# Seven block products for eight in three FFN up-projections (fp32), and FFN down in one pass over eight PSUM banks

## The chip, the cores and the metric

The kernel runs on one core of one Trainium2 chip. The metric is the device time of one execution in microseconds, the median of 3 runs. The engines are called as the profile calls them: PE is TensorE, with PEld its weight loads; DVE is VectorE, ACT is ScalarE, POOL is GpSimd, and SP is the engine whose queue issues the DMAs.

## The reference

Two transformer blocks, the second of two layers, on 512 tokens of width 1024, all in fp32. What the change touches is the feed-forward part, which occurs three times: FFN 0 at the end of the first block, FFN 1 and FFN 2 in the second one, these two with a causal convolution over 3 tokens between.

```
# FFN 0 (D_FF = 2816)
n2 = rmsnorm(h, norm_ffn_pre)
gu = n2 @ w_ffn_in                                  # [512,1024] @ [1024,5632]
ff = (silu(gu[:, :D_FF]) * gu[:, D_FF:]) @ w_ffn_out
h = h + rmsnorm(ff, norm_ffn_post)

# FFN 1 and 2
u = h_normed @ w_up                                 # [512,1024] @ [1024,5632]
y = conv_b + sum(u_padded[j : j + 512] * conv_w[j] for j in range(3))
gate, up = split(y, 2)
x = x + (silu(gate) * up) @ w_down                  # [512,2816] @ [2816,1024]
```

## The kernel before

Every fp32 operand of a matmul is kept as two parts of 12 bits (`split`: ScalarE writes the high part by a copy, VectorE the low part as the difference). A product of two such pairs is `mm3`, three matmuls (lines 108 to 110) into one PSUM bank: high by high, high by low, low by high. The normed and transposed activations X are two tiles, XH and XL, of 8 blocks of 128 channels by 512 tokens.

`projA` computes 256 features of X @ w, feature-major, in two banks: two loads of 512 KB into `raw` (2 buffers), two splits into `whi` and `wlo` (4 buffers each, `RING`), and 16 mm3 of 512 columns. In FFN 0 the split also multiplies by the norm's gain (`split_scaled`, four pieces of 256 a load). A *block* is what one projA computes, and a *pair* f the gate block and the up block of features f and f + 1 (of 22 groups of 128); an FFN has 11 pairs. `gate_sink` and `up_sink` take the results out of the banks: the convolution (`mixed`: one instruction on ScalarE, two on VectorE), silu, the product, and its split into FH and FL, 22 by 512 each. The first pair of each FFN goes through `projA_first`, whose matmuls have 256 columns, so that the last two token tiles are needed late.

`out_proj` is the down projection: `projB` computes the first 512 output columns for all token tiles, in the four rotating banks ("pj"), over 11 chunks of 256 features; then a second pass computes the other 512 columns in the banks c0 to c3, and its last four chunks are taken token tile by token tile, so that `finish` (the residual, the next norm and its transposes) of one tile runs beside the matmuls of the next.

Instructions are issued to in-order queues, one an engine; the framework that builds the program may place an instruction ahead of others of its engine where data and buffers allow. So an eviction that waits for a bank holds up what stands behind it on ScalarE or VectorE. All loads are issued by SP.

## Time and profile before

| | us |
|---|---|
| median of 3 runs (2075.93 to 2077.32) | 2075.95 |
| span of the profiled execution | 2073.6 |
| TensorE busy in it | 2043.1 |
| VectorE busy | 1064.8 |
| ScalarE busy | 847.4 |
| pairs 2 to 11 of FFN 1, 20 blocks | 224.0 |

The profile is of one execution, and its own time is known only by its span, from the first to the last instruction; the median lies 2.35 us above that. Matmuls are pipelined: the duration of one is longer than the distance to the next, so rates are read from starts. FFN 0's up-projection runs from about 440 to 680 us, its down projection to 800; FFN 1 follows the HGRN layer, from about 1127 to 1374 and to 1490; FFN 2 follows the MLA layer, from about 1700 to 1948 and to the end.

### The profile page before, as it was taken

The numbers are of one execution on the slowest core, as the hardware profiler recorded it, in microseconds if no ns is written. First come the engines' busy times: TensorE is split into PE (matmuls) and PEld (weight loads), VectorE is DVE, ScalarE is ACT, GpSimd is POOL, SyncE is SP. The second block draws the span as 40 slices with busy tenths as digits, with TensorE's granted clock in tenths as the row PEclk, the third lists the DMA queues.
The fourth block names the chain that finished last, engine by engine and source line by source line (L and its number), as shares of the span: only waits on it lengthen the run. The fifth ranks groups of instructions, "written<-read, shape, count | busy, mean of one in ns | idle before, by whom it ended". The sixth has DMA issues, their size and how long they took to land.

```text
span 2073.6 us, 26103 instructions
## 1 busy us (share of the span) xinstructions
PE 2043.1 (99%) x10225; PEld 1671.8 (81%) x10225; DVE 1064.8 (51%) x1936; ACT 847.4 (41%) x1649; POOL 55.2 (3%) x84
## 2 busy tenths in 40 slices
PE   8999999999999999999999999999999999999999
PEld 6777778888888888888888888888787788888887
DVE  5664543474443225766555665542466456565421
...
GB/s 219 89 90 72 71 77 127 92 102 92 92 93 99 93 94 79 82 71 63 71 42 77 102 97 96 92 92 101 53 107 41 41 53 100 102 92 92 98 116 61
DMA packets 151362, 182.70 MB, mean 88 GB/s; under 512 B 6983, under 2 KB 118854, under 8 KB 151238
## 3 DMA queue, kind: packets, MB, share of 16 engines
...
q14 instruction: 43, 0.35, 0.0%
HBM read 178.90 MB, written 2.10 MB: 87 GB/s over the span
## 4 chain that ended last, share of the span: by engine, by line
PE 92%; DVE 3%; ACT 2%; DMA 1%; POOL 1%; issue 1%; SPq 0%; POOLq 0%; ACTq 0%; DVEq 0%
PE A L108 17%; PE A L109 17%; PE A L110 17%; PE B L108 10%; PE B L110 10%; PE B L109 9%; PE hs L924 2%; PE zt L86 1%; PE tr L86 1%; PE ov L1013 1%; PE mo L1230 1%; PE mz L1204 1%; POOL r L125 1%; PE sbo L450 1%; PE z L427 1%
## 5 line engine op out<-in xcount | busy, mean ns | idle before, releaser
L108 PE MATMUL A<-XH,whi 128*128 128x512 f32 (+1 forms) x1552 | 590.5, 381 | 0.8 <-ACT XH L62 0.8
L109 PE MATMUL A<-XL,whi 128*128 128x512 f32 (+1 forms) x1552 | 585.4, 377 | 1.5 <-DVE XL L65 1.5
L110 PE MATMUL A<-XH,wlo 128*128 128x512 f32 (+1 forms) x1552 | 584.7, 377 | 0.0
L65 DVE TENSOR_TENSOR wlo<-raw,whi 128x1024 fp32r<-128x1024 f32 (+2 forms) x253 | 301.5, 1193 | 451.9 <-ACT whi L62 451.6
L62 ACT ACTIVATE whi<-raw 128x1024 fp32r<-128x1024 f32 (+2 forms) x253 | 262.1, 1036 | 471.9 <-PE B L110 249.0
L110 PEld LDWEIGHTS A<-XH,wlo 128*128 128x128 f32 x1552 | 293.0, 189 | 58.8 <-issue 0.2
L109 PEld LDWEIGHTS A<-XL,whi 128*128 128x128 f32 x1552 | 293.5, 189 | 57.9 <-DVE XL L65 1.9
L108 PEld LDWEIGHTS A<-XH,whi 128*128 128x128 f32 x1552 | 292.8, 189 | 57.9 <-ACT XH L62 1.3
L108 PE MATMUL B<-whi,FH 128*128 128x512 f32 x528 | 207.2, 392 | 0.0
L110 PE MATMUL B<-whi,FL 128*128 128x512 f32 x528 | 207.0, 393 | 0.0
L109 PE MATMUL B<-wlo,FH 128*128 128x512 f32 x528 | 205.9, 390 | 0.0
L62 ACT ACTIVATE whi<-raw,cols 128x256 fp32r<-128x256 f32 (+1 forms) x272 | 126.8, 525 | 175.4 <-PE A L109 92.4
L68 DVE SCALAR_TENSOR_TENSOR wlo<-raw,cols,whi 128x256 fp32r<-128x256 f32 (+1 forms) x272 | 126.7, 512 | 121.6 <-ACT whi L62 121.3
L68 DVE SCALAR_TENSOR_TENSOR y<-A,convc,y 128x511 f32<-128x511 f32 (+1 forms) x176 | 131.7, 748 | 90.5 <-ACT y L62 87.4
L108 PE MATMUL B<-whi,XH 128*128 128x512 f32 (+2 forms) x416 | 165.8, 400 | 0.0
L109 PE MATMUL B<-wlo,XH 128*128 128x512 f32 (+2 forms) x416 | 158.3, 381 | 2.1 <-DVE wlo L65 1.7
L110 PE MATMUL B<-whi,XL 128*128 128x512 f32 (+2 forms) x416 | 158.0, 381 | 0.0
L109 PEld LDWEIGHTS B<-wlo,FH 128*128 128x128 f32 x528 | 99.1, 188 | 22.2
L110 PEld LDWEIGHTS B<-whi,FL 128*128 128x128 f32 x528 | 99.2, 188 | 21.9
L108 PEld LDWEIGHTS B<-whi,FH 128*128 128x128 f32 x528 | 99.2, 188 | 20.7
L62 ACT ACTIVATE y<-A,convc 128x512 f32<-128x512 f32 x88 | 67.7, 770 | 77.4 <-PE A L110 77.4
L110 PEld LDWEIGHTS B<-whi,XL 128*128 128x128 f32 x416 | 78.5, 189 | 14.9 <-DVE XL L65 0.3
...
## 6 DMA issues: line engine op xcount, KB each, us to landing
...
```

Source lines behind the costliest of these rows:

```text
L62: return nc.scalar.activation(out=out_, in_=in_, func=func, **kw)
L65: return nc.vector.tensor_tensor(out=out_, in0=in0, in1=in1, op=op)
L68: return nc.vector.scalar_tensor_tensor(out=out_, in0=in0, scalar=scalar, in1=in1, op0=op0, op1=op1)
L86: nc.tensor.transpose(dst_bank[:, k * P : (k + 1) * P], s_, ident)
L108: nc.tensor.matmul(out_, lhsT=sta[0], rhs=mov[0], start=first, stop=False)
L109: nc.tensor.matmul(out_, lhsT=sta[0], rhs=mov[1], start=False, stop=False)
L110: nc.tensor.matmul(out_, lhsT=sta[1], rhs=mov[0], start=False, stop=last)
L125: nc.gpsimd.tensor_tensor(out=r, in0=v, in1=mhalf[:, :w], op=ALU.pow)
L427: nc.tensor.matmul(z[:, :n], lhsT=qT[u][r, sl], rhs=kT[v][r, :n], start=u + v == 0, stop=False)
L450: nc.tensor.matmul(b[r, :P], lhsT=sv[:, j, c0 : c0 + 64], rhs=A[:, j * P : (j + 1) * P], start=j == 0, stop=j == i,)
L924: nc.tensor.matmul(b[:, sl], lhsT=K[:, e, sl], rhs=Q[:, e, sl], start=True, stop=True)
L1013: nc.tensor.matmul(b[:, e * P : (e + 1) * P], lhsT=l_, rhs=hv[:, j, hd * P : (hd + 1) * P], start=q == 0, stop=q == len(lhs) - 1,)
```

## The change

Strassen's scheme on 2 x 2 x 2 blocks: 256 features are two halves (`i`), the 1024 channels are the even and the odd groups of 128 (`j`), the 512 tokens two halves of 256 (`l`). `seven` computes a block of 256 features by seven products of [128 features, 512 channels] by [512 channels, 256 tokens] in place of eight. Each product is four mm3 with 256 columns. It needs sums of weight quarters (`usum`, four a block, on VectorE, then split like the quarters that are used as they are) and of activation quarters. Those four (nT1, T3, nT2, T4) are computed once an FFN by `x_sums`, from an unsplit copy of X that `norm_T` now writes as well (`plain`, on ScalarE), and kept split as `xc`. The sums of products are formed partly in the banks (bank Y takes four products one after another, each partial sum copied out by ScalarE; bank XZ takes the others) and partly by VectorE into `dst`.

In FFN 0 gate and up blocks of pairs 2 to 11 are done so; in FFN 1 and 2 the gate blocks, with the up block still a projA whose two parts lie between the pieces of the gate block. The generators' yields lay two blocks side by side. The tiles of `whi` and `wlo` become one ring "w" of 8 tiles of the same size; a product takes one, a split of projA two. The weights of a block of seven come in two loads of [1024, 128] instead of [512, 256], as many bytes. FFN 0's norm takes its gain before the transposes (on VectorE) and its weights are split unscaled. FT is one unsplit fp32 tile; `pair_of` splits it chunk by chunk in the down projection, which takes both column halves in one pass over eight banks.

```diff
-    wp = ctx.enter_context(pool("wp", bufs=RING))
+    wp = ctx.enter_context(pool("wp", bufs=2 * RING))
...
     def chunk(src, nk, n, g=None):
-        """A [nk*128, n] block of a weight matrix (its rows times g) as an exact pair of 12-bit parts."""
         raw = wp.tile([P, nk, n], F32, tag="raw", name=nm("raw"), bufs=2)
         load(raw, src.rearrange("(k p) n -> p k n", p=P))
-        hi = wp.tile([P, nk, n], F32R, tag="whi", name=nm("whi"))
-        lo = wp.tile([P, nk, n], F32R, tag="wlo", name=nm("wlo"))
+        hi = wp.tile([P, nk, n], F32R, tag="w", name=nm("whi"))
+        lo = wp.tile([P, nk, n], F32R, tag="w", name=nm("wlo"))
...
+                act(plain[:, hf * 4 : hf * 4 + 4, c0 : c0 + P], b.rearrange("p (k t) -> p k t", k=4), AF.Copy)
 
...
+            if mid is not None and half.start == 0:
+                mid()
...
+    def mmB(bs, t, c, ch, X, nk, n=512, x0=0):
+            xs_ = X[0][:, kk - x0, sl], X[1][:, kk - x0, sl]
+            mm3(bs[t][:, :n], xs_, (hi[:, k], lo[:, k]), kk == 0, kk == nk - 1)
...
+    def halves_of(T, j, l):
+        return T.rearrange("p (c j) t -> p j c t", j=2)[:, j, :, l * 256 : (l + 1) * 256]
+    def x_sums(X, plain, tmp, xp):
+        B = {(j, l): halves_of(plain, j, l) for j in range(2) for l in range(2)}
+        nT1, T3, nT2, T4 = (tmp[:, 2 * i : 2 * i + 2].rearrange("p k (u t) -> p (k u) t", u=2) for i in range(4))
+        ops = {}
+        def parts(key, src):
+            t_ = [xp.tile([P, 4, 256], F32R, tag="xc", name=nm("xc"), bufs=8) for _ in range(2)]
+            split(src, *t_)
+            ops[key] = t_
+        tt(nT1, B[0, 0], B[0, 1], ALU.subtract)
+        parts("nT1", nT1)
+        tt(T3, B[1, 1], B[0, 1], ALU.subtract)
+        stt(nT2, T3, -1.0, B[0, 0], ALU.mult, ALU.subtract)
+        parts("nT2", nT2)
+        parts("T3", T3)
+        stt(T4, nT2, -1.0, B[1, 0], ALU.mult, ALU.subtract)
+        parts("T4", T4)
+        for j, l in ((0, 0), (1, 0), (1, 1)):
+            ops[j, l] = [halves_of(x_, j, l) for x_ in X]
+        return ops
+    def seven(w, col, ops, xp, dst, c21, done):
+        A = []
+        for i in range(2):
+            raw = (wp, xp)[i].tile([P, KD, P], F32, tag="raw", name=nm("raw"), bufs=2)
+            load(raw, w[:, col + i * P : col + (i + 1) * P].rearrange("(k p) n -> p k n", p=P))
+            A.append([raw.rearrange("p (c j) n -> p j c n", j=2)[:, j] for j in range(2)])
+        bY, bXZ = bank("Y"), bank("XZ")
+        pY, pX, pZ = bY[:, :256], bXZ[:, :256], bXZ[:, 256:]
+        lf, rt = slice(0, 256), slice(256, 512)
+        def product(o, src, key, first):
+            t_ = wp.tile([P, 2, 4, P], F32R, tag="w", name=nm("wu"))
+            split(src, t_[:, 0], t_[:, 1])
+            x_ = ops[key]
+            for c in range(4):
+                mm3(o, (t_[:, 0, c], t_[:, 1, c]), (x_[0][:, c], x_[1][:, c]), first and c == 0, c == 3, skip_group_check=True)
+        def usum(a_, b_, o=None):
+            if o is None:
+                o = xp.tile([P, 4, P], F32, tag="u", name=nm("u"), bufs=2)
+            tt(o, a_, b_, ALU.add)
+            return o
+        product(pY, A[0][0], (0, 0), True)
+        act(dst[0][:, lf], pY, AF.Copy)
+        yield 1
+        u1 = usum(A[1][0], A[1][1])
+        product(pX, u1, "nT1", True)
+        u3 = usum(A[0][0], A[1][0], A[1][0])
+        u2 = usum(u3, A[1][1])
+        product(pY, u2, "nT2", False)
+        act(dst[0][:, rt], pY, AF.Copy)
+        product(pZ, A[0][1], (1, 0), False)
+        tt(dst[0][:, lf], pZ, dst[0][:, lf], ALU.add)
+        done(0, 0)
+        product(pY, u3, "T3", False)
+        act(dst[1][:, rt], pY, AF.Copy)
+        stt(dst[1][:, rt], pX, -1.0, dst[1][:, rt], ALU.mult, ALU.subtract)
+        done(1, 1)
+        yield 1
+        product(pY, A[1][1], "T4", False)
+        c21(dst[1][:, lf], pY)
+        product(pX, usum(u2, A[0][1], u2), (1, 1), False)
+        tt(dst[0][:, rt], pX, dst[0][:, rt], ALU.add)
+        done(0, 1)
...
+    def out_proj(w, Y, nk, gpost, gnext, half0, nxt, plain=lambda: None, parts=None):
...
-        g0 = projB(w, 0, Y, nk, d0)
-        xpool = half0(g0)
-        last = xpool is None
-        Xn = None if last else new_X(xpool)
-        run(g0)
-        bs = [bank("B", f"c{t}") for t in range(NT)]
...
+        else:
+            xpool = half0(None)
+            last = xpool is None
+            Xn = None if last else new_X(xpool)
+            def pair_of(c):
+                y_ = [parts.tile([P, 2, S], F32R, tag="xc", name=nm("yc"), bufs=8) for _ in range(2)]
+                split(Y[:, 2 * c : 2 * c + 2], *y_)
+                return y_
+            b2 = [bank("B") for _ in range(NT)], [bank("B", f"c{t}") for t in range(NT)]
+            bs = b2[1]
+            for c in range(nch - 2):
+                yc = pair_of(c)
+                for hf in range(2):
+                    ch = getB(w, c, hf * 512)
+                    for t in range(NT):
+                        run(mmB(b2[hf], t, c, ch, yc, nk, x0=2 * c))
+            ycs = [pair_of(c) for c in (nch - 2, nch - 1)]
+            ends = [(b2[hf], c, getB(w, c, hf * 512), ycs[c - nch + 2]) for hf in range(2) for c in (nch - 2, nch - 1)]
+        keep = plain()
...
-            for i in range(RING):
-                run(mmB(bs, t, nch - RING + i, ch[i], Y, nk))
+            for i, (bs_, c, ch, yc) in enumerate(ends):
+                run(mmB(bs_, t, c, ch, yc, nk, x0=0 if parts is None else 2 * c))
+                if i == 1 and parts is not None:
+                    d0(t, bs_[t])
...
+    def open_ff(side="left"):
+        F, ff["close"] = open_pool(nm("ff"), side)
+        ff["FT"] = F.tile([P, 22, S], F32, name=nm("FT"))
+    def kept():
+        return ff["FT"][:, 14:22]
...
-    w_fi = (a["w_ffn_in"][0], cols[:, GFC : GFC + KD])
+    w_fi = a["w_ffn_in"][0]
...
-        a["w_out"][0], MG, KD, gain(a["norm_mix_post"][0]), None,
-        lambda g0: XA, ffn_first(w_fi),
+        a["w_out"][0], MG, KD, gain(a["norm_mix_post"][0]), gain(a["norm_ffn_pre"][0]),
+        lambda g0: XA, ffn_first(w_fi), kept,
...
+    def ffn(w_up, w_down, X, steps, xpool, conv, gpost, gnext, nxt, side="left"):
+        FT = ff["FT"]
+        with tc.tile_pool(name=nm("fx"), bufs=1, reuse_waits="tile", side=side) as E:
+            ops = {}
+            def mid():
+                ops.update(x_sums(X, kept(), FT[:, 6:14], E))
+            ff["mid"] = mid
...
+            def gate(f, q, b):
+                act(FT[:, f + q], b if conv is None else mixed(b, f + q), AF.Silu)
+            def up(f, q, b):
+                u_ = b if conv is None else mixed(b, 22 + f + q)
+                tt(FT[:, f + q], FT[:, f + q], u_, ALU.mult)
+            def sink(to, f):
+                def take(bs):
...
+                        to(f, q, bs[q])
+                return take
+            lf, rt = slice(0, 256), slice(256, 512)
+            def gate7(f):
+                if conv is None:
+                    dst = [FT[:, f], FT[:, f + 1]]
+                    def c21(o, src):
+                        act(o, src, AF.Silu, scale=-1.0)
+                    def done(q, l):
+                        if (q, l) == (1, 1):
+                            act(dst[1][:, rt], dst[1][:, rt], AF.Silu)
+                        elif (q, l) == (0, 1):
+                            act(dst[0], dst[0], AF.Silu)
+                else:
+                    dst = [row("g7"), row("g7")]
+                    def c21(o, src):
+                        act(o, src, AF.Copy, scale=-1.0)
+                        gate(f, 1, dst[1])
+                    def done(q, l):
+                        if (q, l) == (0, 1):
+                            gate(f, 0, dst[0])
+                return seven(w_up, f * P, ops, E, dst, c21, done)
...
+            def up7(f):
+                dst = [row("u7"), row("u7")]
+                def c21(o, src):
+                    stt(FT[:, f + 1, lf], src, -1.0, FT[:, f + 1, lf], ALU.mult, ALU.mult)
+                def done(q, l):
+                    if (q, l) == (1, 1):
+                        tt(FT[:, f + 1, rt], FT[:, f + 1, rt], dst[1][:, rt], ALU.mult)
+                    elif (q, l) == (0, 1):
+                        tt(FT[:, f], FT[:, f], dst[0], ALU.mult)
+                return seven(w_up, DFF + f * P, ops, E, dst, c21, done)
...
+                g7 = gate7(f)
+                next(g7)
+                run(tail)
+                next(g7)
+                if conv is None:
+                    tail = up7(f)
+                    next(tail)
+                    run(g7)
+                    next(tail)
+                    u8 = projA(w_up, DFF + f * P, X, sink(up, f))
+                    for _ in range(8):
+                        next(u8)
+                    run(g7)
+                    run(u8)
+            run(tail)
+            r = out_proj(w_down, FT, 22, gpost(), gnext(), lambda g0: xpool, nxt, parts=E)
+        ff["close"]()
+        return r
```

Three places in the order of the instructions. First VectorE in the middle of FFN 0. Before, one pair: the low parts of four weight chunks (wlo), the product with up (y), the low part of the result (FL).

```order
L65 TENSOR_TENSOR y_4065<-y_4065,A_4069 128x512 [waits PE_49]
L65 TENSOR_TENSOR FL_3690<-y_4065,FH_3689 128x512 [waits Activation_49]
L65 TENSOR_TENSOR y_4067<-y_4067,A_4070 128x512 [waits PE_49]
L68 SCALAR_TENSOR_TENSOR wlo_4273<-raw_4270,cols,whi_4272 128x256 [waits DMAHW3_49,Activation_49]
L68 SCALAR_TENSOR_TENSOR wlo_4273<-raw_4270,cols,whi_4272 128x256 [waits Activation_49] x2
L65 TENSOR_TENSOR FL_3690<-y_4067,FH_3689 128x512 [waits Activation_49]
L68 SCALAR_TENSOR_TENSOR wlo_4273<-raw_4270,cols,whi_4272 128x256 [waits Activation_49]
```

After, a third of a pair (u: sums of weight quarters; wu: weight parts, the row writes the low part; XZ: a bank; FT: results):

```order
L65 TENSOR_TENSOR wu_5519<-raw_5513,wu_5519 128x512 [waits PE_49,Activation_49]
L65 TENSOR_TENSOR wu_5535<-raw_5384,wu_5535 128x512 [waits PE_49,Activation_49]
L65 TENSOR_TENSOR wu_5552<-u_5456,wu_5552 128x512 [waits DVE_49,PE_49,Activation_49]
L65 TENSOR_TENSOR FT_3281<-XZ_5259,FT_3281 128x256 [waits PE_49]
L65 TENSOR_TENSOR u_5587<-raw_5515 128x512 [waits DVE_49]
L65 TENSOR_TENSOR wu_5571<-u_5569,wu_5571 128x512 [waits Activation_49]
L65 TENSOR_TENSOR u_5697<-raw_5643 128x512 [waits DMAHW0_49,DVE_49]
L65 TENSOR_TENSOR wu_5589<-u_5587,wu_5589 128x512 [waits Activation_49]
L65 TENSOR_TENSOR raw_5643<-raw_5641,raw_5643 128x4x128 [waits DMAHW7_49,DVE_49]
L65 TENSOR_TENSOR wu_5605<-raw_5513,wu_5605 128x512 [waits PE_49,Activation_49]
```

Sums and low parts stand around the evictions of XZ; a wu row that waits for PE waits for the last reader of its ring tile, the product eight before.

Second, ScalarE at the same place. Before, one silu out of a bank, the high parts of two chunks and one of the result:

```order
L62 ACTIVATE y_4230<-A_4155 128x512 [waits PE_49]
L62 ACTIVATE whi_4357<-raw_4355,cols 128x256 x3
L62 ACTIVATE whi_4399<-raw_4397,cols 128x256 [waits DMAHW6_49,PE_49,Activation_49]
L62 ACTIVATE whi_4399<-raw_4397,cols 128x256 x3
L62 ACTIVATE FH_3689<-y_4228 128x512 [waits DVE_49]
```

After (FT<-Y, u<-Y: a bank copied out; wu: high parts; FT<-FT: silu in place):

```order
L62 ACTIVATE FT_3281<-Y_5258 128x256 [waits PE_49]
L62 ACTIVATE wu_5519<-raw_5513 128x512 [waits DMAHW5_49,Activation_49]
L62 ACTIVATE FT_3281<-FT_3281 128x256 [waits DVE_49]
L62 ACTIVATE u_936_5380<-Y_5386 128x256 [waits PE_49]
L62 ACTIVATE wu_5535<-raw_5384 128x512 [waits Activation_49]
L62 ACTIVATE FT_3281<-Y_5258 128x256 [waits PE_49]
L62 ACTIVATE wu_5552<-u_5456 128x512 [waits Activation_49]
L62 ACTIVATE wu_5571<-u_5569 128x512 [waits PE_49,Activation_49]
```

Copies of bank Y, waiting for TensorE, now stand between the splits.

Third, VectorE at the start of FFN 0, behind the last low part of X. Before, the last two low parts of X and small work for the rotary angles:

```order
L65 TENSOR_TENSOR XL_3281<-tr_3831,XH_3280 128x4x128 [waits Activation_49]
L65 TENSOR_TENSOR XL_3281<-tr_3838,XH_3280 128x4x128 [waits Activation_49]
L65 TENSOR_TENSOR rot_3699<-rot_3697,sinT 128x128 [waits DVE_49]
L65 TENSOR_TENSOR cosT<-cosT,rot_3699 128x128 [waits DVE_49]
L74 TENSOR_SCALAR rot_3697<-angh 128x128
```

After, from the first activation sum (FT<-FT) to the last low part of them:

```order
L65 TENSOR_TENSOR FT_3281<-FT_3281 128x1024 [waits Activation_49]
L65 TENSOR_TENSOR FT_3281<-FT_3281 128x1024
L65 TENSOR_TENSOR rot_3695<-rot_3693,sinT 128x128 [waits DVE_49]
L65 TENSOR_TENSOR xc_3871<-FT_3281,xc_3870 128x1024 [waits Activation_49]
L68 SCALAR_TENSOR_TENSOR FT_3281<-FT_3281 128x1024 [waits DVE_49]
L65 TENSOR_TENSOR wu_3999<-raw_3993,wu_3999 128x512 [waits Activation_49]
L68 SCALAR_TENSOR_TENSOR FT_3281<-FT_3281 128x1024 [waits DVE_49]
L65 TENSOR_TENSOR xc_3877<-FT_3281,xc_3876 128x1024 [waits Activation_49]
L65 TENSOR_TENSOR xc_3881<-FT_3281,xc_3880 128x1024 [waits Activation_49]
L65 TENSOR_TENSOR wu_4017<-u_4015,wu_4017 128x512 [waits PE_49]
L65 TENSOR_TENSOR xc_3886<-FT_3281,xc_3885 128x1024 [waits Activation_49]
```

The four sums, their low parts (xc) and the first two low parts of weights (wu_3999, wu_4017) have come in ahead of the first pair's evictions.

## Rows read from the trace of the kernel before

**Rows 1.** The page: busy time by engine, and the chain that ended last

```profile
PE 2043.1 (99%) x10225; PEld 1671.8 (81%) x10225; DVE 1064.8 (51%) x1936; ACT 847.4 (41%) x1649; POOL 55.2 (3%) x84
...
PE 92%; DVE 3%; ACT 2%; DMA 1%; POOL 1%; issue 1%; SPq 0%; POOLq 0%; ACTq 0%; DVEq 0%
PE A L108 17%; PE A L109 17%; PE A L110 17%; PE B L108 10%; PE B L110 10%; PE B L109 9%; PE hs L924 2%; PE zt L86 1%; PE tr L86 1%; PE ov L1013 1%; PE mo L1230 1%; PE mz L1204 1%; POOL r L125 1%; PE sbo L450 1%; PE z L427 1%
```

**Rows 2.** Busy time by stretch: us, then per engine busy and instructions, clock, DMA

```profile
core 0: us, PE busy (x) PEld busy (x) DVE busy (x) ACT busy (x) POOL busy (x), PEclk, DMA share, GB/s
460.00:680.00 220.00, 220.00 (x945) 177.25 (x944) 90.87 (x189) 87.26 (x189) 0.00 (x0) 1.00 0.31 96
1134.00:1149.00 15.00, 15.00 (x135) 15.00 (x134) 7.07 (x9) 5.08 (x7) 0.00 (x0) 1.00 0.39 117
1156.00:1376.00 220.00, 220.00 (x944) 177.28 (x943) 131.55 (x158) 92.79 (x120) 0.00 (x0) 1.00 0.30 94
1733.00:1950.00 217.00, 217.00 (x932) 174.86 (x931) 128.63 (x154) 91.07 (x118) 0.00 (x0) 1.00 0.30 95
406.00:440.00 34.00, 29.97 (x165) 25.17 (x164) 23.61 (x59) 21.63 (x53) 4.37 (x8) 0.95 0.21 64
```

**Rows 3.** TensorE in order of time, FFN 1: start, duration, engine, line, tiles, form

```profile
1132.77 1.03 PE L86 MATMUL tr<-ident,n 128*128 128x128 f32 x8
...
1139.78 0.28 PE L108 MATMUL A<-XH,whi 128*128 128x256 f32 x1
...
1149.86 0.28 PE L110 MATMUL A<-XH,wlo 128*128 128x256 f32 x1
1149.98 0.39 PE L108 MATMUL A<-XH,whi 128*128 128x512 f32 x1
...
1373.97 0.39 PE L108 MATMUL B<-whi,FH 128*128 128x512 f32 x1
```

**Rows 4.** Groups by line and form: count, busy us and mean ns, idle before

```profile
L65 DVE TENSOR_TENSOR wlo<-raw,whi 128x1024 fp32r<-128x1024 f32 x236 | 288.4, 1223 | 435.0 <-ACT whi L62 434.6
...
L62 ACT ACTIVATE whi<-raw 128x1024 fp32r<-128x1024 f32 x236 | 250.0, 1059 | 457.8 <-PE B L110 247.6 <-PE A L109 168.1 <-issue 18.8
...
L68 DVE SCALAR_TENSOR_TENSOR wlo<-raw,cols,whi 128x256 fp32r<-128x256 f32 x240 | 103.4, 480 | 112.8 <-ACT whi L62 112.6
...
L62 ACT ACTIVATE y<-A,convc 128x512 f32<-128x512 f32 x88 | 67.7, 770 | 77.4 <-PE A L110 77.4
...
L68 DVE SCALAR_TENSOR_TENSOR y<-A,convc,y 128x511 f32<-128x511 f32 x88 | 65.8, 748 | 87.4 <-ACT y L62 87.4
...
L65 DVE TENSOR_TENSOR y<-y,y 128x512 f32<-128x512 f32 x44 | 30.4, 691 | 1.4
...
L65 DVE TENSOR_TENSOR XL<-mo,XH 128x256 fp32r<-128x256 f32 x16 | 6.7, 419 | 15.1 <-ACT XH L62 15.1
...
L62 ACT ACTIVATE XH<-mo 128x256 fp32r<-128x256 f32 x16 | 6.2, 390 | 6.5 <-PE mo L1230 6.5
...
L65 DVE TENSOR_TENSOR wlo<-raw,whi 128x512 fp32r<-128x512 f32 x9 | 6.1, 686 | 15.7 <-ACT whi L62 15.7
...
L62 ACT ACTIVATE whi<-raw 128x512 fp32r<-128x512 f32 x9 | 5.7, 632 | 10.5 <-PE A L109 7.9 <-DMA raw<-in_mla_w_in_dram 1.3 <-PE B L110 0.7
```

**Rows 5.** VectorE in order of time, in the middle of FFN 0

```profile
502.70 0.68 DVE L65 TENSOR_TENSOR FL<-y,FH 128x512 fp32r<-128x512 f32 x1
503.31 0.48 DVE L68 SCALAR_TENSOR_TENSOR wlo<-raw,cols,whi 128x256 fp32r<-128x256 f32 x1
506.86 1.28 DVE L68 SCALAR_TENSOR_TENSOR wlo<-raw,cols,whi 128x256 fp32r<-128x256 f32 x3 [3.08 <-ACT whi L62]
```

**Rows 6.** Chain that ended last: the load of a [1024, 128] weight block, start and us

```profile
41.44 3.85 DMA raw<-in_w_in_dram
```

**Rows 7.** TensorE in order of time at the start of FFN 0, idle before in brackets

```profile
426.75 1.27 PE L86 MATMUL tr<-ident,n 128*128 128x128 f32 x8 [1.47 <-ACT n L62]
...
430.41 0.58 PE L109 MATMUL A<-XL,whi 128*128 128x256 f32 x1 [1.49 <-DVE XL L65]
```

More of the change, by code (lines that the diff above doesn't have):

```diff
@@ L105, in block, with mm3 @@
         return chunk(w[k0 * P : (k0 + nk) * P, col : col + n], nk, n, None if g is None else g[:, k0 : k0 + nk])
-    def mm3(out_, sta, mov, first, last):
-        nc.tensor.matmul(out_, lhsT=sta[0], rhs=mov[0], start=first, stop=False)
-        nc.tensor.matmul(out_, lhsT=sta[0], rhs=mov[1], start=False, stop=False)
-        nc.tensor.matmul(out_, lhsT=sta[1], rhs=mov[0], start=False, stop=last)
+    def mm3(out_, sta, mov, first, last, **kw):
+        nc.tensor.matmul(out_, lhsT=sta[0], rhs=mov[0], start=first, stop=False, **kw)
+        nc.tensor.matmul(out_, lhsT=sta[0], rhs=mov[1], start=False, stop=False, **kw)
+        nc.tensor.matmul(out_, lhsT=sta[1], rhs=mov[0], start=False, stop=last, **kw)
     def split(src, hi, lo):
@@ L150, in norm_T @@
             )
+            if plain is not None:
+                act(plain[:, hf * 4 : hf * 4 + 4, c0 : c0 + P], b.rearrange("p (k t) -> p k t", k=4), AF.Copy)
     def new_X(xp):
@@ L752, in finish @@
                 yield 1
[L753 to L767 removed]
+            yield from norm_T(h[:, t], r, gnext, Xn, t * P, (f"c{t}", f"c{max(t - 1, 0)}"), keep)
+        nch = nk // 2
+        if parts is None:
+            g0 = projB(w, 0, Y, nk, d0)
+            xpool = half0(g0)
+            last = xpool is None
+            Xn = None if last else new_X(xpool)
+            run(g0)
+            bs = [bank("B", f"c{t}") for t in range(NT)]
+            for c in range(nch - RING):
+                ch = getB(w, c, 512)
+                for t in range(NT):
+                    run(mmB(bs, t, c, ch, Y, nk))
+            ends = [(bs, c, getB(w, c, 512), Y) for c in range(nch - RING, nch)]
+        else:
+            xpool = half0(None)
+            last = xpool is None
+            Xn = None if last else new_X(xpool)
+            def pair_of(c):
[8 more added lines that the diff above has]
+                    ch = getB(w, c, hf * 512)
+                    for t in range(NT):
+                        run(mmB(b2[hf], t, c, ch, yc, nk, x0=2 * c))
+            ycs = [pair_of(c) for c in (nch - 2, nch - 1)]
+            ends = [(b2[hf], c, getB(w, c, hf * 512), ycs[c - nch + 2]) for hf in range(2) for c in (nch - 2, nch - 1)]
+        keep = plain()
         fin = []
@@ L848, in ffn @@
+            rot = rotation(E) if conv is None else iter(())
+            tail = iter(())
             for f in range(0, 22, 2):
-                next(side, 0)
-                sg = []
+                next(rot, 0)
                 if f == 0:
-                    sinks[:] = gate_sink(0, sg), up_sink(0, sg)
+                    sinks[:] = sink(gate, 0), sink(up, 0)
                     run(steps)
-                else:
-                    run(projA(w_up, f * P, X, gate_sink(f, sg)))
-                    run(projA(w_up, DFF + f * P, X, up_sink(f, sg)))
@@ L863 @@
         lambda X_, pend: projA_first(w_h, (D, 0), X_, (lambda b: sinks[0](b), lambda b: sinks[1](b)), pend),
+        "right",
     )
@@ L1037, in hgrn_half0 @@
         pools["RB"] = open_pool("RB", "right")
+        open_ff("right")
         return pools["RB"][0]
-    X, steps = out_proj(a["hgrn_w_out_2"][0], OT, KD, None, gain(a["norm_ffn_2"][0]), hgrn_half0, ffn_first(a["ffn_w_up_2"][0]))
+    X, steps = out_proj(a["hgrn_w_out_2"][0], OT, KD, None, gain(a["norm_ffn_2"][0]), hgrn_half0, ffn_first(a["ffn_w_up_2"][0]), kept)
     RB, close_RB = pools["RB"]
@@ L1263, in mla_half0 @@
         pools["XC"] = open_pool("XC")
+        open_ff()
         return pools["XC"][0]
-    X, steps = out_proj(a["mla_w_out_2"][0], OT, KD, None, gain(a["norm_ffn_2"][1]), mla_half0, ffn_first(a["ffn_w_up_2"][1]))
+    X, steps = out_proj(a["mla_w_out_2"][0], OT, KD, None, gain(a["norm_ffn_2"][1]), mla_half0, ffn_first(a["ffn_w_up_2"][1]), kept)
     XC, close_XC = pools["XC"]
```

42 lines of the change are left out of this document (7 added, 35 removed).

## The prediction

> **What bounds the kernel now.** I read the busy times first, then the chain of work that ended last, then the stretches of the three FFN up-projections. TensorE is busy 99% of the span and the chain is TensorE for 92% of it, most of that in the matmuls of lines 108 to 110 [rows 1]. In the up-projections TensorE has no gap at all: 220.00 of 220 us in FFN 0 and FFN 1, 217.00 of 217 in FFN 2, while VectorE is at 41%, 60% and 59% there [rows 2]. So a matmul less is time less, until VectorE or ScalarE, which the change loads, end last. A busy TensorE is not yet TensorE at its rate, so I take start-to-start times. The 20 blocks of FFN 1 after its first pair run from 1149.98 to 1373.97 [rows 3]: 224 us for 20 x 48 matmuls of 512 columns, 0.2333 us each, 11.20 us a block. Matmuls of 256 columns with the same two-part weights stand at the start of each FFN: from 1139.78 to 1149.86 there are 89 steps in 10.08 us [rows 3], 0.1133 us each. Two halves take 0.2267, a little less than one whole, so cutting the token axis in two costs nothing by itself.
>
> **The removed and the added matmuls.** A block of eight is 16 mm3, 48 matmuls of 512. A block of seven is 7 products x 4 x 3 = 84 matmuls of 256: 84 x 0.1133 = 9.52 us, 1.36 us a product. Gain 11.20 - 9.52 = 1.68 us a block. FFN 0 does both halves (gate and up) of pairs f = 2 to 20 in this way, 20 blocks; FFN 1 and FFN 2 only the gate, 10 blocks each. 40 x 1.68 = 67.2 us off TensorE, 33.6 of it in FFN 0. The matmuls of the down projections are as many as before.
>
> The Trainium skill (TensorE: Matmul & The Clock Gate, Back-to-back issue gap) gives 518 cycles between matmuls at 512 columns and 262 at 256; by that the gain would be 48 x 518 - 84 x 262 = 2856 cycles, 1.19 us a block and 48 us in all, an estimate from that page. The trace does not agree on the wide ones (0.2333 us is 560 cycles at 2.4 GHz, 0.1133 is 272), and the rows decide.
>
> **FFN 0, one pair (14 products, 14 x 1.36 = 19.04 us of TensorE).** VectorE before: 90.87 of 220 us [rows 2]. After, a pair has 14 low parts of 512 (0.686 each), 8 sums of 512 (0.691, the row of an addition of that size), 5 operations of 256 (0.419), 3 scalar_tensor_tensor of 256 (0.480) and one of 512 (0.691) [rows 4]: 9.60 + 5.53 + 2.10 + 1.44 + 0.69 = 19.36 us, just over the 19.04. But those are whole durations, and instructions that wait for nothing start sooner: 502.70 to 503.31 is 0.61 for one of 0.68, and three of 256 with a column take 1.28, 0.40 a step [rows 5]. At such steps it is 23 x 0.61 + 5 x 0.419 + 3 x 0.40 = 17.3 us, 91%. The truth lies between; a VectorE that is late doesn't wait and so goes by the steps, so I take it as full but not the bound. ScalarE: 14 high parts of 0.632, 8 pieces of 256 (0.390) and a silu of 512 (about 0.632) [rows 4], 12.6 us: no bound.
>
> Waits in the new order. Ring "w" has 8 tiles and a product takes one, so each split waits for the end of the product eight before and is needed seven products, 9.5 us, later; the order of after shows the splits ahead of the evictions by that much. A late split is thus covered. Three things have less cover. Bank Y must be copied by ScalarE (0.390) between two products into it with one product (1.36) between: enough. XZ is read by a scalar_tensor_tensor behind that copy, with two products (2.72) before the next write; walking the pair with these durations, VectorE is done with it 1.4 us ahead. And the second weight half has two buffers: the one for the next up block is free some 12.7 us into the pair (after the low part for product 9 of its last user) and VectorE wants the new contents at 15.8. A load of this shape took 3.85 us [rows 6], so VectorE is held 0.8 us at its queue's head, with an eviction of XZ behind it, and 0.6 us of the 1.4 remain. I take 0 to 0.35 us a pair lost (19.36 - 19.04), 0 to 3.5 in all, and put down 1.
>
> **FFN 1 and 2, one pair (9.52 + 11.20 = 20.72 us).** VectorE: 7 x 0.686 + 4 x 0.691 + 2 x 1.223 + 2 x 0.419 + 0.480 + 8 x 0.748 (the convolution) + 2 x 0.691 = 18.7 us by whole durations [rows 4], 90%. ScalarE: 7 x 0.632 + 2 x 1.059 + 4 x 0.390 + 4 x 0.770 + 2 x 0.632 = 12.4. The wide block in two parts between the products gives each wait 5.6 us of cover. Loss 0.
>
> **Starts of the FFNs.** x_sums stands between the last token tile's split and product 2. Behind that split TensorE has 96 matmuls of 256, 10.9 us, and product 1. In FFN 0 VectorE does, up to product 3's low part, two differences and two combinations of 1024 (four of about 1.22), four low parts of 1024, three of 512, two products with up and some small rotation work: 8 x 1.22 + 5 x 0.69 + 1.2 = 14.4 us, after some 1.2 us for ScalarE's plain copies; that is 15.6 against 10.9 + 2.7 + 0.2 = 13.8 and about 1 us of lead: 1 to 2 us of idle TensorE. Before, this entry had idled it 4 us with the clock at 0.95 [rows 2], the transposes waiting for ScalarE's norm and a matmul for a low part of X [rows 7]; the plain copies and the gain, now on VectorE, lie in that chain: 0 to 2 us. In FFN 1 the last transposes stand at 1132.77 and end 16.2 us before the first wide matmul [rows 3], 5.3 more than the 10.9 of the second half; with the splits of X off, the lead is some 4 us, against 8 x 0.748 = 6.0 us of convolution for the first pair: about 1 us, and as much in FFN 2. Bounds for all three: -1 (FFN 0's weight splits no longer carry a gain, 4 x 0.480 become 1.223) to 12 us; I put down 4.5.
>
> **Down projections.** The splits of FT move from the sinks to pair_of, 11 of 1024 (1.059 and 1.223) for 22 of 512, beside 11.2 us of matmuls a chunk: nothing. A junction can hold the first B matmul for the first two splits, 2.3 us less the three products (4.1 us) that still run; the last bank is waited for 0 to 2 us. The tail squares or adds the first half beside the second half's 2.8 us. I put down 0.5 each, 1.5 in all, bounds 0 to 6. SP issues as many bytes as before, one gain more.
>
> **Sum.** On the profiled execution's span of 2073.6: -67.2 + 1 + 4.5 + 1.5 = -60.2, 2013.4; the median of 2075.95 lies 2.35 above that span, so 2015.8, say 2016 us. Own range from the bounds: 2008 (no loss) to 2030.
>
> **Rivals.** *VectorE or its loads end last in FFN 0.* For it: 19.36 against 19.04, and 0.6 us of margin behind a load. If it pays whole durations and is held 0.8 us twice a pair, a pair takes 21.0 us, 10 pairs lose 19, and the time is 2034; with loads of 5 us, some 2 us a pair more at most, 2055. Against it: the steps of [rows 5], and an in-order engine that is late stops waiting.
> By the Trainium skill (VectorE: DVE Perf Modes, Terms) a flush follows each operation and the next can't issue before it is empty, which is whole durations. The steps of 0.61 for 0.68 speak against it here.
> *Weight loads bind the products.* In the 256-column stretch the weight loads are busy 15.00 of 15 us [rows 2]. There weights lie split long before; should fresh weight tiles cost more, half the gain is gone at 0.1233 us a matmul: 2050. Against: TensorE is equally busy there, and at the same form, address pattern and order of three.
> *Slower: queue heads reach TensorE.* 280 products share 67.2 us, so it decides at 0.24 us a product, and 0.26 would be 0.3% slower. If the copy of a product stood ahead of the next split on ScalarE with no lead, a product would wait 0.390 + 0.632 + 0.686 = 1.7 us, less the 0.23 of its first two matmuls: 280 x 1.5 = 420 us, 2430 us. That needs fewer than two products between split and use. Against: seven lie between.
> *It doesn't do what it says:* if the last evictions of each block stay uncovered (Y, then XZ, 1 us on each of 40 blocks) some 20 to 27 of the 67 us remain, 2055; the interleaving of two blocks speaks against it.
>
> **Chances.** Forecast (2008 to 2030) 0.72; VectorE or loads in FFN 0 0.17; weight loads 0.03; uncovered evictions 0.03; slower 0.05. Range for 8 in 10: 2008 to 2036, all of the forecast's and the near half of the first rival. A measurement of this kernel can tell about 0.2% (4 us) from no change: faster 0.94, within 0.01, slower 0.05.
>
> **What the profile after would show.** Steps of 0.113 us in lines of Y and XZ, 84 of them a block, right; more, and the weight loads bind. TensorE busy near 100% from pair 2 on in all three FFNs; if FFN 0 is below 97% with idle ended by VectorE, the first rival is right, and VectorE above 95% there says whether by work or, below it, by loads. Idle of 1 to 4 us at each FFN's start ended by xc or wu. A pair of FFN 0 should take 19.0 to 19.4 us, of FFN 1 and 2 20.7. I am wrong if a pair of FFN 0 takes over 20.5 us or a start idles over 5.

## The result, and the profile after

The changed kernel takes 2028.8 us (median), the kernel before 2075.9 in the same rounds: ratio 0.978, 95% interval 0.977 to 0.980. It is faster, by 47 us, where 60 were forecast (2016, range 2008 to 2036). Its profiled execution took 2036.45 us, 7.7 above its median: TensorE stood at a granted clock of 0.86 between 1480 and 1530 us, in the stage between FFN 1 and 2. For the sum below I therefore also use a second profiled execution of the same kernel (after_again), with a span of 2026.8 us and a clock of 1.00 there.

The page after (compare [rows 1]): busy time by engine, and the chain that ended last.

```profile
PE 1990.5 (98%) x11665; PEld 1701.7 (84%) x11665; DVE 1277.1 (63%) x2293; ACT 958.0 (47%) x1862; POOL 56.4 (3%) x84
...
PE 80%; DVE 9%; DMA 5%; ACT 3%; issue 2%; POOL 1%; SPq 0%; DVEq 0%; POOLq 0%; ACTq 0%
```

TensorE is still the bound of the whole, but the chain has lost 12 points of it, to VectorE and to loads. Where, the stretches show (they answer to [rows 2]; same columns): FFN 0's pairs, FFN 1's and FFN 2's from the second pair of seven on, and the starts of FFN 1 and FFN 2.

```profile
core 0: us, PE busy (x) PEld busy (x) DVE busy (x) ACT busy (x) POOL busy (x), PEclk, DMA share, GB/s
454.00:645.00 191.00, 185.16 (x1599) 182.82 (x1599) 170.81 (x329) 109.95 (x226) 0.00 (x0) 1.00 0.37 106
1140.00:1338.00 198.00, 197.41 (x1246) 176.05 (x1245) 165.67 (x247) 114.07 (x184) 0.00 (x0) 1.00 0.36 106
1712.00:1909.00 197.00, 197.00 (x1247) 176.02 (x1246) 164.50 (x246) 113.56 (x183) 0.00 (x0) 1.00 0.34 102
1112.00:1140.00 28.00, 25.13 (x205) 24.18 (x204) 25.77 (x35) 14.78 (x23) 0.00 (x0) 1.00 0.22 65
1682.00:1712.00 30.00, 26.29 (x202) 25.34 (x201) 27.36 (x37) 17.72 (x27) 0.00 (x0) 0.94 0.26 77
```

FFN 1 and 2 run as forecast once they run: 197.41 of 198 and 197.00 of 197 us, a pair 20.7 us. FFN 0 does not: 185.16 of 191, 96.9%, its 19 blocks from 456.21 to 647.23 take 10.05 us each for 9.52, a pair 20.1 us. And the two starts stand idle for 2.9 and 3.7 us.

**FFN 0.** The chain of waits in FFN 0, 515 to 600 us: start, us, what.

```profile
by line: DMA raw<-in_w_ffn_in_dram 37.0%; DVE wu L65 19.6%; issue 11.8%; DVE u L65 7.8%; DVE raw L65 6.3%; ACT wu L62 2.5%; DVE FT L68 2.0%; ACT FT L62 1.6%; DVE u L68 1.6%; PE Y L110 1.6%; PE Y L108 1.6%; PE Y L109 1.6%; ACT u L62 1.3%; PE
...
526.91 3.87 DMA raw<-in_w_ffn_in_dram
...
532.09 0.69 DVE raw L65
...
535.62 1.28 DVE wu L65 x2
536.93 4.00 DMA raw<-in_w_ffn_in_dram
...
546.79 3.81 DMA raw<-in_w_ffn_in_dram
```

TensorE is hardly in it. The chain is a loop: a load of a second weight half (3.9 us); VectorE's first sum of it, at 530.88 us; behind that sum in VectorE's queue six us of sums and splits, up to the low part (`wu`, to 536.9) that frees the buffer of the block before; the next load (536.93). One turn is 9.9 us, more than the 9.52 of a block. Who waits there, 515 to 650 us, TensorE and then VectorE (us in total, times, longest):

```profile
PE XZ L108 <- DVE u L68: 2.3, 5, 0.7
PE XZ L108 <- DVE FT L68: 2.1, 2, 1.9
...
DVE u L65 <- DMA raw<-in_w_ffn_in_dram: 13.0, 11, 1.8
```

And the hold before the longest wait of TensorE (VectorE; idle before in brackets):

```profile
520.96 0.69 DVE L65 TENSOR_TENSOR u<-raw 128x512 f32<-128x512 f32 x1 [1.79 <-DMA raw<-in_w_ffn_in_dram]
```

That is the chain which the prediction walked (VectorE held at a load, an eviction of XZ behind it). The mean of 1.2 us a hold hides two kinds: holds of 1.6 to 1.8 us (at 520.96, 530.88, 550.70, 570.37, 590.07, 610.34 and 629.98 us) and between them holds of 0.2 to 0.8. Behind each long one TensorE comes late some 4 us on, by 0.3 us or more. So the 1.4 us of lead that the prediction gave VectorE were about right, and the hold was twice the forecast 0.8.

**The starts of FFN 1 and 2.** VectorE in order of time at FFN 1's start, and the longer of TensorE's two idle rows there.

```profile
1115.79 0.69 DVE L65 TENSOR_TENSOR raw<-raw,raw 128x512 f32<-128x512 f32 x1 [2.16 <-DMA raw<-in_ffn_w_up_dram]
1116.40 2.35 DVE L65 TENSOR_TENSOR FT<-FT 128x1024 f32<-128x1024 f32 x2
...
1125.67 1.22 DVE L65 TENSOR_TENSOR xc<-FT,xc 128x1024 fp32r<-128x1024 f32 x1
1126.81 2.71 DVE L68 SCALAR_TENSOR_TENSOR y<-A,convc,y 128x511 f32<-128x511 f32 x4
...
1129.01 0.36 PE L108 MATMUL Y<-XH,wu 128*128 128x256 f32 x1 [2.22 <-DVE y L68]
```

x_sums begins late, behind a sum that waits 2.16 us for a weight load, and ends at 1126.9; only then come the convolutions of the first pair's gate, which free the banks that the first product of seven takes. I had put the convolutions (6 us) against the lead, but not the order: they stand behind all of x_sums. At FFN 2's start TensorE's two waits are for the same convolutions (`y`) and for ScalarE's copy of bank Y (`g`):

```profile
PE Y L108 <- ACT g L62: 2.0, 1, 2.0
PE Y L108 <- DVE y L68: 1.7, 1, 1.7
```

### The profile page after: what moved, and what is told of

It reads as the page before. It is cut to its first block, busy times and chain, and to the rows that moved or that the text cites. A ratio compares the mean times of both kernels' runs of the same rounds, so it can differ in the third digit from the quotient of the medians.

```text
span 2034.6 us, 29719 instructions
## 1 busy us (share of the span) xinstructions
PE 1990.5 (98%) x11665; PEld 1701.7 (84%) x11665; DVE 1277.1 (63%) x2293; ACT 958.0 (47%) x1862; POOL 56.4 (3%) x84
## 4 chain that ended last, share of the span: by engine, by line
PE 80%; DVE 9%; DMA 5%; ACT 3%; issue 2%; POOL 1%; SPq 0%; DVEq 0%; POOLq 0%; ACTq 0%
PE B L108 10%; PE B L110 10%; PE B L109 10%; PE A L108 9%; PE A L109 9%; PE A L110 8%; PE hs L1099 2%; DVE wu L65 2%; PE Y L108 2%; PE Y L109 2%; PE Y L110 2%; DMA raw<-in_w_ffn_in_dram 2%; PE XZ L108 2%; PE XZ L109 2%; PE XZ L110 2%
## 5 line engine op out<-in xcount | busy, mean ns | idle before, releaser
L108 PE MATMUL A<-XH,whi 128*128 128x512 f32 (+1 forms) x912 | 337.1, 370 | 0.2 <-ACT XH L62 0.2
L109 PE MATMUL A<-XL,whi 128*128 128x512 f32 (+1 forms) x912 | 332.4, 365 | 0.8 <-DVE XL L65 0.8
L110 PE MATMUL A<-XH,wlo 128*128 128x512 f32 (+1 forms) x912 | 331.7, 364 | 0.0
L110 PE MATMUL B<-whi,yc 128*128 128x512 f32 x528 | 208.0, 395 | 0.0
L108 PE MATMUL B<-whi,yc 128*128 128x512 f32 x528 | 207.6, 393 | 0.0
L109 PE MATMUL B<-wlo,yc 128*128 128x512 f32 x528 | 207.3, 393 | 0.0
L110 PEld LDWEIGHTS A<-XH,wlo 128*128 128x128 f32 x912 | 173.1, 190 | 29.5 <-issue 0.2
L109 PEld LDWEIGHTS A<-XL,whi 128*128 128x128 f32 x912 | 173.3, 190 | 26.4 <-DVE XL L65 1.2
L108 PEld LDWEIGHTS A<-XH,whi 128*128 128x128 f32 x912 | 172.8, 190 | 26.8 <-ACT XH L62 0.7
L108 PE MATMUL Y<-xc,wu 128*128 128x256 f32 x480 | 133.8, 279 | 5.0 <-ACT g L62 3.2
L110 PE MATMUL Y<-xc,wu 128*128 128x256 f32 x480 | 133.0, 277 | 0.0
L109 PE MATMUL Y<-xc,wu 128*128 128x256 f32 x480 | 132.9, 277 | 0.0
L110 PEld LDWEIGHTS B<-whi,yc 128*128 128x128 f32 x528 | 99.4, 188 | 21.8
L108 PEld LDWEIGHTS B<-whi,yc 128*128 128x128 f32 x528 | 99.4, 188 | 21.8 <-issue 0.4
```

What stands on the lines that cost most here:

```text
L108: nc.tensor.matmul(out_, lhsT=sta[0], rhs=mov[0], start=first, stop=False, **kw)
L109: nc.tensor.matmul(out_, lhsT=sta[0], rhs=mov[1], start=False, stop=False, **kw)
L110: nc.tensor.matmul(out_, lhsT=sta[1], rhs=mov[0], start=False, stop=last, **kw)
```

## The ledger

I count as lost what a step from one matmul's start to the next exceeds its rate (0.2333 or 0.1133 us), from the last transposes of an FFN's entry to its first down matmul; for most waits this is 0.2 us more than the idle row, since the first two steps after a wait are longer too. On the second execution (2026.8 - 2073.6 = -46.8):

| term | forecast | found |
|---|---|---|
| 40 blocks x 1.68 | -67.2 | -67.2 |
| FFN 0, first 75 us | +2.5 | +2.3 |
| FFN 0, pairs after that | +1 | +7.0 waits, +2.1 slower rate |
| start of FFN 1 | +1 | +3.5 waits, +0.3 slower rate |
| start of FFN 2 | +1 | +3.4 waits, +1.5 at 1.2 GHz, +0.1 more at the slower rate than before |
| down projections and the rest | +1.5 | +0.2 (what remains) |
| sum | -60.2 | -46.8 |

The slower rate is a second pace of the 256-column matmuls, of which more below. The same count for all runs (us lost; in FFN 1 and 2, what was lost at 1.2 GHz after the plus):

| run | FFN 0, 75 us | FFN 0, rest | FFN 0, slower rate | FFN 1 waits | FFN 2 waits |
|---|---|---|---|---|---|
| changed, profiled | 2.6 | 7.2 | 1.3 | 4.6 | 4.3 + 1.6 |
| after_again | 2.3 | 7.0 | 2.1 | 3.5 | 3.4 + 1.5 |
| third_buffer | 1.9 | 1.2 | 0.2 | 4.2 | 4.0 + 1.6 |
| third_again | 1.9 | 0.7 | 5.4 | 3.3 | 3.6 + 1.6 |
| no_last_sum | 2.7 | 0.9 | 5.5 | 2.0 | 3.9 |
| no_sums | 3.1 | 0.8 | 5.8 | 0.1 | 0.1 |
| free_banks | 2.1 | 4.5 | 3.5 | 4.0 | 3.2 + 1.6 |
| sums_gpsimd | 6.6 | 3.7 | 2.8 | 4.6 + 2.9 | 5.4 + 2.4 |
| sums_order | 2.7 | 7.2 | 0.7 | 4.1 | 4.4 |
| order_third | 1.4 | 0.9 | 5.5 | 4.9 | 5.3 |
| later_third | 1.4 | 1.4 | 0.8 | 1.5 | 1.2 |

## Experiments

The code lines are shortened.

**The down part alone (eight_one_pass).** `gate7` and `up7` replaced by `projA`, x_sums not called.

> Every block by eight products as before, no x_sums, and the rest of the change kept: FT in one part, FFN down in one pass over 8 banks, the gain of FFN 0 in the norm. This prices that part of the change by itself. Theory (as forecast, the down projections and junctions cost 0 to 2 us): 2074 to 2078, beside 2075.9 of before. Rivals: the one pass loses 1 us or more at each junction, 2079 and more; or it gains (the splits of FT off the sinks), 2072 and less.

Measured: 2076.65 us, ratio 1.0003 (0.9994 to 1.0012). FFN 0's down projection became 1.0 us longer up to its first transposes (0.3 up to its last), its up projection 0.9 shorter. The theory holds: one pass over eight banks is free within what can be measured, and the gain and loss lie in the blocks of seven and x_sums, which this run leaves out.

**A third buffer for the second weight half (third_buffer).**

```
+ if i == 1 and spare is not None: raw = spare
+ def third(n):   # n: block of FFN 0
+     return FT[:, 20:22] (as 8 x 128) if conv is None and n % 3 == 2 and n < 15
```

> Nothing is left out; in FFN 0 every third block's second weight half is loaded into rows 20 and 21 of FT, which are free until pair 20, so the half has three buffers for two up to pair 16. In the changed kernel VectorE stands 13.2 us in FFN 0 behind these loads, and TensorE loses 6.7 us after the third pair, each time to an XZ product whose bank a late VectorE operation frees. Theory (the loads hold VectorE's queue): these 6.7 us go for 15 of 20 blocks, about 5 us, 2024 (2022 to 2025). Rival (VectorE's own work, 17.3 to 19.4 us of each 19.0 us pair, is the bound): within 1.5 us of 2028.8.

Measured: 2024.9 us (0.976, 0.973 to 0.978). In its profile FFN 0's waits after the first 75 us fell from 7.0 or 7.2 to 1.2 us, the up projection by 7.7 us (214.2 to 206.5), and what was left of the holds (515 to 650 us):

```profile
DVE u L65 <- DMA raw<-in_w_ffn_in_dram: 2.5, 2, 1.5
```

So loads held FFN 0, not the amount of VectorE's work, which is the same here. The gain of the median is smaller than that of the profile, and the second run of the kernel shows why.

> The kernel with the third buffer in FFN 0, once more. Its first profile had all of FFN 0 at 0.1133 us a 256-column matmul, waits of 3.1 us there (1.2 after the first 75 us), and 2023.5 us. Theory: the waits come again within 1 us, whatever the rate; the time follows the rate, 2019 to 2021 where all stretches are fast and 2027 to 2030 where FFN 0 is slow (1596 matmuls x 0.0044 = 7 us). Rival (the rate is of the program): the profile is fast in the same stretches as before.

Measured: 2026.2 us, 0.8 below the forecast for a slow FFN 0; 0.7 us of waits in FFN 0 after the first 75 (1.2 in the first profile). But the rate had changed. Busy time of 550 to 640 us in the two executions, third_buffer and then third_again, the same instructions in the same order:

```profile
550.00:640.00 90.00, 90.00 (x796) 90.00 (x796) 79.14 (x143) 55.12 (x108) 0.00 (x0) 1.00 0.34 100
```

```profile
550.00:640.00 90.00, 90.00 (x766) 90.00 (x766) 78.09 (x141) 53.03 (x105) 0.00 (x0) 1.00 0.34 98
```

796 matmuls against 766 in 90 us at the same granted clock: 0.1133 and 0.1177 us a step. The rate belongs to the execution, not to the program. The second run of the changed kernel (after_again, 2029.4 us) says the same: its slower stretches in FFN 0 lie elsewhere (440 to 475, 483 to 495 and 505 to 511 us, for 544 to 556 and 634 to 651), while the waits come again, at 9.3, 3.5 and 3.4 us for 9.8, 4.6 and 4.3.

**The last sum left out (no_last_sum).** `product(pX, u2, ...)` for `product(pX, usum(u2, A[0][1], u2), ...)`.

> Left out: the last of the four weight sums of each block of seven (the last product takes the third sum's result), 40 additions of 512, 20 of them in FFN 0, 0.61 to 0.69 us each, 12 to 14 us of VectorE's work in FFN 0. Theory (loads hold VectorE from the fourth pair on, backlog of x_sums before): only the backlog shrinks, 0 to 3 us, 2026 to 2029. Rival (VectorE's work is the bound in FFN 0): 6 to 9 us go there, 2020 to 2023.

Measured: 2025.5 us, between the two. In its profile most of FFN 0 ran at the slower rate (5.5 us lost), at which a block takes 9.9 us, as long as a turn of the loop of loads. TensorE then hardly waits (0.9 us), whatever VectorE does, so this run can't tell; third_buffer did.

**x_sums left out (no_sums).**

```
- ops.update(x_sums(X, kept(), FT[:, 6:14], E))
+ ops.update(halves of X for (0, 0), (1, 0), (1, 1)); nT1, nT2, T3, T4 = the same halves
```

> Left out: the sums and differences of X and their splits at the start of each FFN (x_sums' 4 operations and 4 splits of 1024); the products that wanted them take halves of X instead, so the matmuls are as many. In the changed kernel TensorE loses 4.4 us over the first two pairs of FFN 1, 5.8 in FFN 2 (1.6 of it at a lower clock) and 2.5 in the first three pairs of FFN 0. Theory (these losses are VectorE's backlog behind x_sums): nearly all of it goes, 2028.8 - 12.7 = 2016, at most 2019. Rival (the first pair's convolutions and the first weight loads hold the start in any case): less than 3 us goes, 2026 or more. Neither touches FFN 0's losses after its third pair.

Measured: 2022.7 us (0.974, 0.973 to 0.976), above the 2019 that the theory allowed. The starts of FFN 1 and FFN 2 without it:

```profile
1115.00:1140.00 25.00, 25.00 (x191) 23.92 (x190) 20.50 (x31) 13.62 (x22) 0.00 (x0) 1.00 0.32 93
1675.00:1700.00 25.00, 25.00 (x196) 23.89 (x195) 20.78 (x31) 14.34 (x23) 0.00 (x0) 1.00 0.31 93
```

No wait and no lower clock in either: the theory holds there. It fails for FFN 0, whose first 75 us lose as much as before (3.1), so that loss isn't x_sums'; and part of the gain was eaten by the slower rate (5.8 us in FFN 0, 4.4 in FFN 1).

**Other banks, other order (free_banks, sums_order).** Two ways to take the convolutions off the path: give the first block banks of its own, or put the convolutions ahead of x_sums' second half.

```
+ gate7, f == 2: bank("Y", "c0"), bank("XZ", "c1")                                  # free_banks
+ with tc.issue_after(last convolution of the gate): split T3; T4; split T4         # sums_order
+ with tc.issue_after(nT1): u3 = usum(...)                                          # sums_order
```

> Nothing is left out; the first block of seven of each FFN takes its two PSUM banks from the transposes' banks c0 and c1, which are free, in place of banks of the first pair's gate. So its first product waits for no convolution. In the changed kernel it waited 2.44 us in FFN 1 and 1.92 in FFN 2, and the third product 0.87 and 2.23 for ScalarE's copy of Y. Theory (VectorE's backlog, 10 us of x_sums ahead of the convolutions, is the cause, and ScalarE's copy of Y is queued behind a silu that waits for them): the first wait only moves to the third product; the sum of waits stays at 4.1 to 4.6 us in FFN 1 and 3.8 to 4.3 in FFN 2, time within 1 us of the changed kernel's. Rival (the banks are the cause): 2.4 and 1.9 us go, 4.3 us less in all.

> Nothing is left out and no work is added or taken; only VectorE's queue at the starts of FFN 1 and 2 is in another order: the convolutions of the first pair's gate stand ahead of x_sums' second half (the split of T3, T4 and its split, which products 5 and 6 need), and the sum that waits for the second weight load stands behind x_sums' first subtraction. Theory (the gate's convolution and the copy of Y come late because 10 us of x_sums and a held load stand ahead on VectorE): TensorE's waits fall from 3.5 to 4.6 us to 1 or less in FFN 1, from 3.4 to 4.3 to 1 or less in FFN 2, and with them the stretch at 1.2 GHz there (1.5 us); in all 6 to 8 us, 2022. Rival (any order of the same work is late somewhere, as with the other banks): the wait turns up at the fourth to sixth product, the sums stay above 3 us, 2027 and more.

Measured: 2027.7 and 2031.3 us; the changed kernel takes 2028.8 to 2029.4. Neither gains more than 2 us. TensorE's waits in FFN 1, in free_banks and then in sums_order (whose lines stand one lower):

```profile
PE Y L108 <- ACT g L62: 1.7, 3, 1.1
PE XZ L110 <- DVE wu L65: 1.1, 1, 1.1
```

```profile
PE Y L109 <- ACT g L63: 1.5, 2, 1.1
PE XZ L111 <- DVE wu L66: 1.0, 1, 1.0
```

The row `Y <- DVE y` of 2.2 us is gone in both, and the time with it is not: the product behind now waits for a low part, and the third for ScalarE's copy of Y. That copy is queued in free_banks behind a silu that waits for a convolution, in sums_order behind the high part of T4, which waits for VectorE's T4. For free_banks I had expected this; for sums_order I had not. My theory of the order was wrong. What is left is the amount of VectorE's and ScalarE's work ahead of the first blocks of seven, which no_sums bears out and later_third tests below; which of the two engines' work it is, no run separates.

**Work moved to GpSimd (sums_gpsimd).** nT1 and T4 (as two additions) by `nc.gpsimd.tensor_tensor`.

> Nothing is left out; of x_sums' four operations of 1024 the first and the last (as two additions) are done by GpSimd in place of VectorE. No trace so far has an operation of that size on GpSimd. Theory (backlog on VectorE): VectorE is relieved of 2 x 1.22 = 2.4 us at each start, and the waits fall from 4.6 to about 2.2 us in FFN 1 and from 4.3 to about 2 in FFN 2; 2024 us. Rival (GpSimd's operation takes over 4 us, or slows VectorE's beside it): the second or the sixth product waits for it in place, the sum of the waits is as before or more; 2029 or more.

Measured: 2045.7 us, 17 slower than the changed kernel. The rival was right by its second way: GpSimd's operations take 2.4 to 3.5 us, not over 4, but VectorE's beside them are slowed. GpSimd at FFN 1's start, and VectorE beside it (start, duration, idle before in brackets):

```profile
1122.32 2.39 POOL L293 TENSOR_TENSOR FT<-FT 128x1024 f32<-128x1024 f32 x1 [7.81 <-ACT FT L62]
1126.54 2.72 POOL L300 TENSOR_TENSOR FT<-FT 128x1024 f32<-128x1024 f32 x1 [1.83 <-DVE FT L65]
```

```profile
1123.25 2.02 DVE L65 TENSOR_TENSOR raw<-raw,raw 128x512 f32<-128x512 f32 x1 [1.63 <-DMA raw<-in_ffn_w_up_dram]
...
1126.92 3.42 DVE L68 SCALAR_TENSOR_TENSOR FT<-FT 128x1024 f32<-128x1024 f32 x1
```

VectorE's sum took 2.02 us for 0.69, its combination 3.42 for 1.23: they end 0.6 and 1.1 us after the GpSimd operations beside them (at 1124.71 and 1129.26), which is about their own length. They did not run in parallel, and GpSimd takes twice VectorE's time for the same. An operation with one input in PSUM (`y<-B,r,g`, at 431.14 us, beside a GpSimd operation from 431.07) took its usual 0.75 us. The two profiled executions lie 14.5 us apart (spans of 2041.3 and 2026.8). Some 9 us of that are in the table. Another 3 lie ahead of it: the framework put T4's first addition beside the norm of the last token tile, where VectorE's two `n` operations took 3.55 us for 1.41 in FFN 1 and as much in FFN 2, and each of the three entries became 1.0 us longer. TensorE was also more often at 1.2 GHz, 35.5 us of the span in all for 16.0 in after_again. The Trainium skill (SBUF — State Buffer, Terms) says that the two engines share a pair of ports, held for a whole instruction, and that the loser fully blocks; the trace agrees (2.02 us for 0.69, 3.42 for 1.23).

**The sums where they are covered (later_third, order_third).** In FFN 1 and 2 the second pair by eight products, x_sums behind the first pair's convolutions; with the third buffer. order_third is sums_order with the third buffer.

```
+ if f == 2 and conv is not None: gate by projA
+ with tc.issue_after(last convolution of the first pair): ops.update(x_sums(...))
```

> Nothing is left out. In FFN 1 and 2 the gate of the second pair is done by eight products as before the change, and x_sums stands on VectorE behind the convolutions of the whole first pair, with some 20 us of TensorE's work over it; FFN 0 has the third buffer for the second weight half. Price: 2 x 1.68 = 3.4 us of TensorE. Theory (what costs at the starts of FFN 1 and 2 is the work of VectorE and ScalarE ahead of the first block of seven, in whatever order): the waits fall from 3.4 to 4.6 us to under 1 in each, the up projections take 190.4 - 9 x 1.68 shorter than by eight... that is, from the last transpose to the first down matmul, 227.15 and 229.03 us become about 225.5 each. With FFN 0 as with the third buffer alone the time is 2028.8 - 7 - 1.6 - 3.5 = 2017 where 256-column matmuls stand 0.1133 us apart, up to 2027 where they stand 0.1177. Rival (the first block of seven is late wherever it stands): waits above 3 us come again behind the second pair, 2025 and more, in the faster stretches too.

> Nothing is left out: the new order of VectorE's queue in FFN 1 and 2 together with the third buffer for the second weight half in FFN 0. Theory (two separate losses, so they add): 6 to 8 us from the starts and 6 to 7.5 from FFN 0 (waits 9.3 to 9.8 down to about 3), 2028.8 - 13.5 = 2015, 2012 to 2019; the loss against the count of matmuls is then some 3 us in FFN 0, 1 each in FFN 1 and 2. Rival (what is won at one place is given back in a lower clock or in 256-column matmuls at 0.1177 us): 2020 and more.

Measured: later_third 2018.4 us (0.972, 0.971 to 0.974), order_third 2026.0 (0.975, 0.973 to 0.977). The two starts of later_third, FFN 1 and then FFN 2:

```profile
PE Y L108 <- ACT g L62: 1.1, 1, 1.1
...
PE Y L108 <- ACT g L62: 0.3, 1, 0.3
PE A L110 <- DVE wlo L65: 0.2, 1, 0.2
```

The waits fell to 1.5 and 1.2 us (under 1 expected) and the spell at 1.2 GHz in FFN 2 is gone, for 3.4 us of matmuls: 226.8 and 226.6 us from the last transpose to the down projection, some 1.2 more than expected. This is the fastest version, 10.4 us below the change; the third buffer alone gave 2.6 and 3.9 us in its two runs. order_third missed its 2012 to 2019 (one of its five executions took 2015.5) and is no proof that the two gains add: its starts didn't improve (4.9 and 5.3 us), and its FFN 0 ran at the slower rate.

## Why the prediction was right, and where its sum was off

- **The removed and added matmuls: right.** A product takes 1.36 us, a block of seven 9.52, a wide block 11.20 (its halves 5.60). The weight loads don't bind at the faster rate. The gap that the Trainium skill gives for isolated 256-column matmuls (TensorE: Matmul & The Clock Gate, Back-to-back issue gap), 262 cycles, isn't reached after the change either: 272, and 282 at the slower rate. So the estimate of 48 us that the prediction worked out from that page lies beside the measured 47 by chance: the matmuls gave 67, and waits and the slower pace took 20 back.
- **FFN 0's pairs: the term was mis-sized, 7 for 1, and 2 more came from a pace that no term had.** The named chain was the right one, but its margin was walked once, from the moment at which a buffer is free, with one load of 3.85 us. In the trace it is a loop: the low part that frees a buffer stands behind the held sum in the same queue, so a hold makes the next load late. Load 3.8 to 4.4 us, then the sum within 0.1 us of the landing, then 6.0 us to the release make a turn of 9.9 for a block of 9.52. By the forecast's own sign (FFN 0 below 97%, idle ended by VectorE, VectorE below 95% busy: loads) the first rival was right, at half its price: 20.1 us a pair for the 21.0 I gave it. That VectorE's steps go by 0.60 for a 0.68 us operation held: it did the pairs of third_buffer in 19 us.
- **Starts of FFN 1 and 2: mis-sized, 2 for 9.** I compared the convolutions with the lead and left out what stands ahead of them on the same queue. So the sign was wrong as well: the idle was to be ended by `xc` or `wu`, and it was ended by the convolution (`y`) and by the copy of Y (`g`). In the profiled execution FFN 2's start lost 5.9 us, 3.7 of them idle; I had named an idle of over 5 as wrong.
- **Start of FFN 0: the number right, 2.3 for 2.5, by luck.** 1 to 2 us of it were to be lost at products 2 and 3, behind x_sums. There the trace has 0.1 us. The waits of the first 75 us stand at 471 and 482 us, for ScalarE's copies of Y (454 to 646 us), and without x_sums as much is lost (3.1):

```profile
PE Y L108 <- ACT u L62: 0.7, 1, 0.7
PE Y L108 <- ACT FT L62: 0.6, 1, 0.6
```

The longer entry, which the same term priced at 0 to 2 us, came: from the first to the last transposes of the four token tiles 21.6 us for 20.1. It lies ahead of the ledger's stretch and so in its last row, with entries of FFN 1 and 2 that became 0.4 and 0.5 us shorter.
- **Down projections: right** (about 0 for 1.5). The other rivals (weight loads, queue heads, uncovered evictions) did not happen.

That the time fell into the forecast's own range (2008 to 2030) is partly luck. FFN 0's pairs lost 9.1 us where its bounds allowed 3.5; the starts lost 11.1 of their 12, and the down projections left nearly all of their 6 unused. That the change would be faster was never in doubt.
